# A hybrid decoder layer on one core: norm and rotation of a projection put between the next projection's products, and half of the first expert query put behind the first head's keys

## The chip, the core and the metric

The kernel runs on one core of a Trainium2 chip, as one launch. The metric is the device time of that launch in microseconds (us), taken as the median of several runs. The core has five engines with a queue of instructions each, which they work off in order: PE (TensorE, matmuls), DVE (VectorE), ACT (ScalarE), POOL (GpSimd) and SP (SyncE, which here only issues transfers). Transfers between the memory of the chip (HBM) and the core run on 16 DMA engines, whoever issued them. An instruction waits for others through semaphores.

## The reference

256 positions of width 1024 go through one layer. In short:

```python
h = rms_norm(x, attn_norm)
mq, mk, mv, dq, dk, dv = split(h @ w_in)               # six projections of 512 columns each
mq, mk, dq, dk = apply_rope(rms_norm(.., gain), cos, sin)   # per head of 64
a = moba_attention(mq, mk, mv)                          # 8 heads x 64, causal within 256
b = diff_attention(dq, dk, dv, lam)                     # 4 heads, (softmax1 - lam softmax2) V
x = x + concat(norm(a), norm(b)) @ w_out
# PEER: for each token 8 heads x 16 experts of 16384
q   = (xn @ w_query).reshape(.., 8, 2, 128)             # xn = rms_norm(x, ffn_norm)
sc  = einsum(q, sub_keys);  top_s, top_i = top_k(sc, 16)
best = top_k(top_s[0][:, None] + top_s[1][None], 16)    # 16 experts per head
act = gelu(xn . expert_down[e]);  x = x + sum(softmax(best) * act * expert_up[e])
```

## The kernel before

The 256 tokens are two blocks of 128, A and B. A token's place in its block is its partition. For block A everything up to the expert lists is computed first. Then the experts of A are fetched and added, one *slot* after another, and the attention of block B is computed in between, so that B's lists are there when A's experts are through. There are 256 slots, 128 for each block: a slot takes the same list position for all 128 tokens.

**A slot.** `issue()` puts an indirect transfer (a *gather*, line 605) on POOL's queue: it fetches for each token one row of 2048 floats, the down and the up vector of an expert, into a buffer `uv`, one MB in all. `dot()` (line 615) multiplies the down half with the token on DVE and sums it. `weigh()` (lines 621, 622, 627) makes gelu, gate and a diagonal matrix `dg` of the result on ACT. `add()` (line 639) multiplies `dg` with the up half on PE, into `acc`. In every fourth slot of block A the addition is on DVE instead (line 637). After that the buffer is free and `issue()` puts the next gather into it. So the number of buffers limits how many gathers are under way: four at first (`RING0`), five more (`gat1`) once the projections of block B are done and their memory is free, six more (`gat2`) once the attention of B is done. I count the gathers from 0.

**Lists.** `query()` (line 478) makes the queries of two heads (four products of 128 columns, 16 instructions each); `keys()` (line 489) multiplies one head's query with the keys; `route1()` and `route2()` search the 16 experts of a head on DVE (lines 511 to 576), and `ready` says how many gathers the lists allow. `choose(A, 0, 0, 1)` makes the first head's list, with which the first 16 gathers can start; `choose(A, 0, 1, 1)` makes the second head's.

**Block B in between.** A projection is `proj()` (line 185), eight products on PE into one bank `psB`, and `evac()`: ACT copies and squares the result (lines 196, 198), DVE sums the squares (201) and makes the inverse root in eleven small instructions (`rsqrt`, lines 124 to 134), POOL and DVE multiply with the rotation tables (215 on POOL, 217 on DVE), POOL adds the two (220) and DVE scales (222). The last three together with the root I call the *norm and rotation* of a projection. `turn()` (line 229) transposes the result on PE. The projections are numbered 5, 4 (values), 2, 3 (a key and a query), 0, 1 (the other query and key). Weights come in four tiles of 512 KB per projection through a ring of eight tiles (`WRING`), issued on SP by `fetch`.

**What sets the order.** Up to `manual_schedule()` a scheduler orders the instructions on each engine. From there on they stand as the program writes them: the main loop takes a slot, then so many steps of the generator `behind()` as `STEPS` says (four at first), and a step is what a generator does up to its next `yield`. `behind()` mixes the second head's list with `front()`, which holds projections 3, 0 and 1 of block B and then its attention.

## Time and profile before

| what | us |
|---|---|
| median of 3 runs (851.11 to 854.19) | 852.66 |
| the profiled execution | 848.25 |
| its span, first to last instruction | 846.5 |

PE is busy for 80% of the span, DVE for 63%, POOL for 48% and ACT for 35%. The profile page has a line that gives the mean busy share of the DMA engines in 40 slices of the span: it is 9 tenths or more in most of them, with a dip in the fourth and fifth slice (about 63 to 106 us) and another in the eighth and ninth (about 148 to 190 us). A row of a timeline gives the start, the duration, the engine, the source line, the operation with what it writes and reads, and in brackets how long its engine had been idle and what ended that.

### The profile page before, as it was taken

The numbers are of one execution on the slowest core, as the hardware profiler recorded it, in microseconds if no ns is written. First come the engines' busy times: TensorE is split into PE (matmuls) and PEld (weight loads), VectorE is DVE, ScalarE is ACT, GpSimd is POOL, SyncE is SP. The second block draws the span as 40 slices with busy tenths as digits, with TensorE's granted clock in tenths as the row PEclk, the third lists the DMA queues.
The fourth block names the chain that finished last, engine by engine and source line by source line (L and its number), as shares of the span: only waits on it lengthen the run. The fifth ranks groups of instructions, "written<-read, shape, count | busy, mean of one in ns | idle before, by whom it ended". The sixth has DMA issues, their size and how long they took to land.

```text
span 846.5 us, 8001 instructions
## 1 busy us (share of the span) xinstructions
PE 679.3 (80%) x2028; PEld 323.8 (38%) x2028; DVE 535.0 (63%) x1417; ACT 299.9 (35%) x907; POOL 410.4 (48%) x438
## 2 busy tenths in 40 slices
PE   6999987776988958986668767699787877878776
PEld 2454633253654723543425333244222222222222
DVE  4754566757878798676596868774454544545444
ACT  1331232313645534233243333443333333333332
POOL 3310343465447537455538384755555555555530
PEclk9999998878897989998898999889999999999999
DMA  9992798669899999999999999999999999999993
GB/s 350 352 356 91 244 409 332 230 263 406 302 395 376 369 409 382 420 417 419 420 418 420 417 419 420 421 420 420 420 418 421 420 421 418 420 421 420 420 419 155
DMA packets 51534, 318.93 MB, mean 377 GB/s; under 512 B 6113, under 2 KB 6369, under 8 KB 18593
## 3 DMA queue, kind: packets, MB, share of 16 engines
q0 software_dynamic: 36944, 268.85, 78.0%
q1 hardware_dynamic: 14112, 48.93, 15.2%
q10 hardware_dynamic: 432, 0.66, 0.2%
q8 instruction: 16, 0.26, 0.1%
q14 instruction: 30, 0.24, 0.1%
HBM read 317.36 MB, written 1.05 MB: 376 GB/s over the span
## 4 chain that ended last, share of the span: by engine, by line
DMA 43%; PE 31%; DVE 16%; issue 4%; ACT 3%; POOL 2%; DVEq 0%; POOLq 0%; SPq 0%; ACTq 0%
DMA uv<-in_uv_dram,eid 41%; PE acc L639 10%; PE psB L185 7%; PE psA L478 5%; DVE uv L615 5%; PE psB L353 3%; PE psA L255 1%; DMA w<-in_win_dram 1%; DVE x L637 1%; PE psA L489 1%; DMA w<-in_wout_dram 1%; DVE topi L514 1%; POOL uv L605 1%; DVE topi L523 1%; DVE s L517 1%
## 5 line engine op out<-in xcount | busy, mean ns | idle before, releaser
L639 PE MATMUL acc<-uv,dg 128*128 128x512 f32 x896 | 455.3, 639 | 129.2 <-ACT dg L627 123.5
L605 POOL DMA_INDIRECT uv<-in_uv_dram,eid x256 | 316.7, 1237 | 312.4 <-DMA uv<-in_uv_dram,eid 141.6
L615 DVE SCALAR_TENSOR_TENSOR uv<-uv,xn 128x1024 f32<-128x1024 f32 x256 | 311.1, 1227 | 163.7 <-DMA uv<-in_uv_dram,eid 161.2
L639 PEld LDWEIGHTS acc<-uv,dg 128*128 128x128 f32 x896 | 163.8, 199 | 379.2 <-ACT dg L627 233.6
L621 ACT ACTIVATE hdot<-hdot 128x1 f32<-128x1 f32 x256 | 51.3, 200 | 322.9 <-DVE uv L615 321.8
L627 ACT ACTIVATE dg<-ident,hdot 128x128 f32<-128x128 f32 x224 | 89.9, 401 | 21.2 <-PE acc L639 14.4
L185 PE MATMUL psB<-w,xT 128*128 128x512 f32 x192 | 89.8, 617 | 6.9 <-DMA w<-in_win_dram 6.9
L622 ACT ACTIVATE hdot<-hdot,gate 128x1 f32<-128x1 f32 x256 | 75.4, 294 | 8.3
L478 PEld LDWEIGHTS psA<-xgT,w 128*128 128x128 f32 x512 | 69.4, 207 | 21.3 <-issue 20.3
L478 PE MATMUL psA<-xgT,w 128*128 128x128 f32 x512 | 69.3, 289 | 0.0
L185 PEld LDWEIGHTS psB<-w,xT 128*128 128x128 f32 x192 | 37.2, 199 | 51.1 <-issue 49.1
L499 POOL TENSOR_TENSOR ci<-tf 128x4 f32<-128x4 f32 (+5 forms) x81 | 27.8, 375 | 55.6 <-DVE tf L527 55.5
L637 DVE SCALAR_TENSOR_TENSOR x<-uv,hdot,x 128x1024 f32<-128x1024 f32 x32 | 41.7, 1303 | 5.2 <-ACT hdot L622 5.2
L571 DVE TENSOR_REDUCE ef<-hit 128x16 f32<-128x320 f32 (+3 forms) x18 | 12.0, 670 | 37.5 <-POOL hit L557 37.5
L353 PE MATMUL psB<-w,mT 128*128 128x512 f32 x64 | 30.8, 610 | 2.7 <-DMA w<-in_wout_dram 2.7
L557 POOL TENSOR_TENSOR hit<-hit,ci 128x160 f32<-128x160 f32 (+1 forms) x32 | 27.0, 873 | 2.9 <-DVE hit L554 2.5
L215 POOL TENSOR_TENSOR qt<-pr,rS 128x128 f32<-128x128 f32 (+1 forms) x24 | 15.6, 675 | 24.1 <-ACT pr L196 24.0
L511 DVE MAX8 tops<-sc 128x8 f32<-128x128 f32 x32 | 7.2, 281 | 30.3 <-ACT sc L490 30.3
L615 DVE DVE_READ_ACCUMULATOR uv<-uv,xn 128x1 f32 x256 | 20.9, 82 | 0.0
L353 PEld LDWEIGHTS psB<-w,mT 128*128 128x128 f32 x64 | 12.0, 194 | 17.4 <-issue 13.2
L196 ACT ACTIVATE pr<-psB,r 128x512 f32<-128x512 f32 x8 | 5.5, 685 | 36.8 <-PE psB L185 31.2
L482 ACT COPY qs<-psA 128x512 f32<-128x512 f32 (+1 forms) x9 | 4.8, 536 | 36.6 <-PE psA L478 36.6
(126 smaller groups left out, 424.9 us busy)
## 6 DMA issues: line engine op xcount, KB each, us to landing
w<-in_win_dram SPq DMA_DIRECT2D x40, 512.0 KB, 7.3
w<-in_wq_dram SPq DMA_DIRECT2D x28, 512.0 KB, 11.8
w<-in_wout_dram SPq DMA_DIRECT2D x16, 512.0 KB, 11.3
uv<-in_uv_dram,eid POOLq DMA_INDIRECT x256
sk<-in_sk_dram SPq DMA_DIRECT2D x1, 1024.0 KB
out_dram<-x SPq DMA_DIRECT2D x4, 256.0 KB
xT<-in_xT_dram SPq DMA_DIRECT2D x2, 256.0 KB
x<-in_x_dram ACTq DMA_DIRECT2D x1, 512.0 KB
```

The costliest lines, as they stand in the source:

```text
L185: PE.matmul(p, lhsT=xT[tt][:, k], rhs=W[ci, tt][k // 2][:, k % 2], start=(k == 0), stop=(k == KC - 1))
L353: PE.matmul(wops[tt, n], lhsT=mixT[tt, MOBA if k < 4 else DIFF][:, k % 4], rhs=W["o", n, tt][k // 2][:, k % 2], start=(k == 0), stop=(k == ...
L478: PE.matmul(p[:, c], lhsT=w[k // 2][:, k % 2, c * P:(c + 1) * P], rhs=xgT[tt][:, k], start=(k == 0), stop=(k == KC - 1))
L499: eng.tensor_tensor(d, src[:, :, 1, b0:b0 + nb], src[:, :, 0, a0:a0 + 1].to_broadcast([P, src.shape[1], nb]), op=OP.add)
L557: G.tensor_tensor(e[:, h], e[:, h], ci[:, h, None, :n].to_broadcast([P, 8, n]), op=OP.mult)
L605: G.indirect_dma_start(out=rows[n], out_offset=None, in_=uv_d, in_offset=bass.IndirectOffsetOnAxis(ap=eid[tt][:, k:k + 1], axis=0))
L615: V.scalar_tensor_tensor(uv[:, :D], uv[:, :D], 1.0, xn[n // NSEL], op0=OP.mult, op1=OP.mult, accum_out=h)
L621: S.activation(h, h, AF.Gelu)
L622: S.activation(h, h, AF.Copy, scale=gate[n // NSEL][:, col:col + 1])
L627: S.activation(dg, ident, AF.Copy, scale=h)
L637: V.scalar_tensor_tensor(x2[tt], uv[:, D:], dg, x2[tt], op0=OP.mult, op1=OP.add)
L639: PE.matmul(acc[tt][:, c], lhsT=dg, rhs=uv[:, D + c * 512:D + (c + 1) * 512], start=(k == 0), stop=(k == NSEL - 1))
```

## The change

Three things are written in another order; no arithmetic is added or removed.

1. The first `query` is run for two of its four products, then the first head's list is made, and then the other two products are computed. The weights of the next query are fetched behind that.
2. The weights of projections 3, 0 and 1 of block B are fetched by lines of their own, ahead of where `project` had fetched them.
3. In `front()`, the steps of projection 0's products alternate with the steps of `evac` of projection 3 (and its turns), and those of projection 1's products with `evac` of projection 0. Only `evac` of projection 1 stands alone behind its products.

```diff
     load_q(0, wqp)
-    run(query(A, 0, ((0, 2), (2, 4))))
+    q0 = query(A, 0, ((0, 2), (2, 4)))
+    for _ in range(4):
+        next(q0)
+    run(choose(A, 0, 0, 1))
+    run(q0)
     load_q(1, wqp)
-    run(choose(A, 0, 0, 1))
...
     def project(g):
-        if g < 4:
+        if g == 2:
             fetch((g, B), win_d[g], wts)
         else:
             W[g, B] = W[g, A]
         yield from proj(g, B)
         yield from evac(g, B)
-        if g in (3, 1):
-            turn(g - 1, B)
-            yield
-            turn(g, B)
-            yield
 
     run(project(5), project(4), project(2))
+    fetch((3, B), win_d[3], wts)
+    fetch((0, B), win_d[0], wts)
...
-        for g in (3, 0, 1):
-            yield from project(g)
+
+        def turned(g):
+            yield from evac(g, B)
+            if g == 3:
+                turn(2, B)
+                yield
+                turn(3, B)
+                yield
+
+        yield from proj(3, B)
+        fetch((1, B), win_d[1], wts)
+        for g in (0, 1):
+            p, e = proj(g, B), turned(3 if g == 0 else 0)
+            next(p)
+            yield
+            for _ in p:
+                yield
+                next(e, None)
+                yield
+            for _ in e:
+                yield
+        yield from evac(1, B)
+        turn(0, B)
+        yield
+        turn(1, B)
+        yield
```

On SP's queue all rows stand as before: the transfers of the weights keep their places in the built program, although the lines that fetch them have moved. What moves is on the other engines. In the rows, `x2` is a count, and the numbers behind names tell buffers apart.

PE, from the last products of projection 3 (`psB_922`) on, before the change; `psB_1040` is projection 0, the two rows L229 are the turns of projections 2 and 3, and each L639 row is the add of a gather, here gathers 2, 3, 4 and 6:

```order
L185 MATMUL psB_922<-w_918,xT1_104 128x512 x2
L185 MATMUL psB_922<-w_920,xT1_104 128x512 x2
L639 MATMUL acc_935<-uv_899,dg_949 128x512 x2
L639 MATMUL acc_935<-uv_901,dg_966 128x512 x2
L229 MATMUL psA_1008<-ident_117,qo_880 128x128 x4
L229 MATMUL psA_1015<-ident_117,qo_989 128x128 x4
L639 MATMUL acc_935<-uv_938,dg_1000 128x512 x2
L185 MATMUL psB_1040<-w_1032,xT1_104 128x512 x2
L185 MATMUL psB_1040<-w_1034,xT1_104 128x512 x2
L185 MATMUL psB_1040<-w_1036,xT1_104 128x512 x2
L639 MATMUL acc_935<-uv_970,dg_1065 128x512 x2
```

The same place after the change, where projection 3 is `psB_930` and projection 0 is `psB_972`:

```order
L185 MATMUL psB_930<-w_893,xT1_104 128x512 x2
L185 MATMUL psB_972<-w_895,xT1_104 128x512
L639 MATMUL acc_943<-uv_915,dg_957 128x512 x2
L185 MATMUL psB_972<-w_895,xT1_104 128x512
L185 MATMUL psB_972<-w_897,xT1_104 128x512
L639 MATMUL acc_943<-uv_917,dg_980 128x512 x2
L185 MATMUL psB_972<-w_897,xT1_104 128x512
L639 MATMUL acc_943<-uv_946,dg_998 128x512 x2
L185 MATMUL psB_972<-w_899,xT1_104 128x512 x2
L185 MATMUL psB_972<-w_901,xT1_104 128x512
L229 MATMUL psA_1068<-ident_117,qo_880 128x128 x4
L639 MATMUL acc_943<-uv_984,dg_1060 128x512 x2
```

Seven of projection 0's eight products now stand ahead of the turns, and the add of gather 4 (`uv_946`) stands ahead of both turns.

DVE, around the norm of projection 0 (it begins with L201), before the change; `uv_1030` is gather 8, and the dot of gather 9 (`uv_1068`) follows eleven rows of the root, two of L217 and the three small rows L545, L547 and L549 further down:

```order
L538 MAX best_1098<-cs_1047 128x8
L540 MAX_INDEX pos_1099<-best_1098,cs_1047 128x8
L542 MATCH_REPLACE s3_1100<-best_1098,cs_1047 128x50
L615 SCALAR_TENSOR_TENSOR uv_1030,hdot_1104<-uv_1030,xn0_653 128x1024
L201 TENSOR_REDUCE ssq_1114<-sq_1096 128x8
L124 TENSOR_SCALAR rs_v_1117<-ssq_1114 128x8
```

The same place after the change; the dot of gather 9 reads `uv_1063`:

```order
L538 MAX best_1104<-cs_1042 128x8
L540 MAX_INDEX pos_1105<-best_1104,cs_1042 128x8
L542 MATCH_REPLACE s3_1106<-best_1104,cs_1042 128x50
L615 SCALAR_TENSOR_TENSOR uv_1030,hdot_1110<-uv_1030,xn0_653 128x1024
L545 MAX best_1104<-s3_1106 128x8
L547 MAX_INDEX pos_1105<-best_1104,s3_1106 128x8
L549 CAST posf_1128<-pos_1105 128x16
L615 SCALAR_TENSOR_TENSOR uv_1063,hdot_1130<-uv_1063,xn0_653 128x1024
L201 TENSOR_REDUCE ssq_1138<-sq_1123 128x8
```

The dot of gather 9 and the three small rows of the second list have moved ahead of the norm of projection 0.

POOL, from the gathers into the first freed buffers on, before the change (L605 are gathers 4 to 8):

```order
L605 DMA uv_938<-in_uv_dram,eid0_672 128x2048
L605 DMA uv_952<-in_uv_dram,eid0_672 128x2048
L605 DMA uv_970<-in_uv_dram,eid0_672 128x2048
L215 TENSOR_TENSOR qt_990<-pr_956,rS1_817 128x8x32 x2
L605 DMA uv_1004<-in_uv_dram,eid0_672 128x2048
L220 TENSOR_TENSOR qo_989<-qo_989,qt_990 128x512
L605 DMA uv_1030<-in_uv_dram,eid0_672 128x2048
```

The same place after the change:

```order
L605 DMA uv_946<-in_uv_dram,eid0_672 128x2048
L605 DMA uv_960<-in_uv_dram,eid0_672 128x2048
L605 DMA uv_984<-in_uv_dram,eid0_672 128x2048
L605 DMA uv_1002<-in_uv_dram,eid0_672 128x2048
L605 DMA uv_1030<-in_uv_dram,eid0_672 128x2048
L215 TENSOR_TENSOR qt_1034<-pr_987,rS1_817 128x8x32 x2
```

Gathers 7 and 8 now stand ahead of the rotation of projection 3; the sum of that rotation (L220) stands further down, behind the twelve small rows of the second list and behind gather 9. Up to the first gather into the five new buffers, POOL issues 17 gathers before the change and 18 after it.

## Rows read from the trace of the kernel before

**Rows 1.** The page: span; DMA queues with packets, MB and share of 16 engines' span.

```profile
span 846.5 us, 8001 instructions
...
q0 software_dynamic: 36944, 268.85, 78.0%
q1 hardware_dynamic: 14112, 48.93, 15.2%
```

**Rows 2.** Busy time by stretch: length, engines (instructions), then PE clock, DMA share, GB/s.

```profile
102.00:138.00 36.00, 27.09 (x65) 11.96 (x64) 23.52 (x71) 11.20 (x28) 15.72 (x15) 0.91 1.00 401
138.00:180.00 42.00, 30.09 (x69) 13.27 (x69) 28.58 (x68) 12.18 (x31) 22.85 (x34) 0.87 0.60 205
...
204.00:232.00 28.00, 24.32 (x108) 15.64 (x107) 23.57 (x57) 15.67 (x41) 15.79 (x20) 0.83 0.88 330
...
300.00:818.00 518.00, 403.98 (x1046) 174.23 (x1045) 325.80 (x791) 186.72 (x598) 284.45 (x278) 0.95 1.01 417
```

**Rows 3.** Timeline: the first query, the first head's keys, and gather 0.

```profile
85.18 7.46 PE L478 MATMUL psA<-xgT,w 128*128 128x128 f32 x64
...
92.48 0.61 PE L489 MATMUL psA<-sk,qs 128*128 128x128 f32 x4
...
102.27 1.05 POOL L605 DMA_INDIRECT uv<-in_uv_dram,eid  x1 [1.68 <-DMA w<-in_win_dram]
```

**Rows 4.** Timeline: the copy of projection 2, and the add of gather 0.

```profile
110.36 0.69 ACT L196 ACTIVATE pr<-psB,r 128x512 f32<-128x512 f32 x1 [6.24 <-PE psB L185]
...
114.32 1.98 PE L639 MATMUL acc<-uv,dg 128*128 128x512 f32 x4 [1.03 <-ACT dg L627]
```

**Rows 5.** Timeline of POOL: issues of gathers 8, 9, 17 and 18.

```profile
137.34 0.96 POOL L605 DMA_INDIRECT uv<-in_uv_dram,eid  x1 [6.31 <-DVE x L637]
141.36 0.96 POOL L605 DMA_INDIRECT uv<-in_uv_dram,eid  x1 [0.16 <-issue]
...
178.69 1.95 POOL L605 DMA_INDIRECT uv<-in_uv_dram,eid  x1 [0.30 <-issue]
180.94 0.94 POOL L605 DMA_INDIRECT uv<-in_uv_dram,eid  x1 [0.30 <-issue]
```

**Rows 6.** Timeline of PE: turn 3, adds 4 and next, projection 0.

```profile
132.87 1.08 PE L229 MATMUL psA<-ident,qo 128*128 128x128 f32 x4 [5.20 <-DVE qo L222]
133.75 3.62 PE L639 MATMUL acc<-uv,dg 128*128 128x512 f32 x4
...
137.16 5.92 PE L185 MATMUL psB<-w,xT 128*128 128x512 f32 x12
```

**Rows 7.** Timeline of DVE: dots 3, 4, 8, 9, 12; sums (L201) of projections 0 and 1.

```profile
122.97 1.23 DVE L615 SCALAR_TENSOR_TENSOR uv<-uv,xn 128x1024 f32<-128x1024 f32 x1 [0.46 <-DMA uv<-in_uv_dram,eid]
...
129.93 2.18 DVE L615 SCALAR_TENSOR_TENSOR uv<-uv,xn 128x1024 f32<-128x1024 f32 x1
...
142.84 1.23 DVE L615 SCALAR_TENSOR_TENSOR uv<-uv,xn 128x1024 f32<-128x1024 f32 x1 [2.60 <-DMA uv<-in_uv_dram,eid]
...
147.91 0.69 DVE L201 TENSOR_REDUCE ssq<-sq 128x8 f32<-128x512 f32 x1 [3.84 <-ACT sq L198]
...
148.83 1.93 DVE L125 TENSOR_SCALAR rsq<-rs_v 128x8 int32<-128x8 int32 x1
...
154.82 1.21 DVE L615 SCALAR_TENSOR_TENSOR uv<-uv,xn 128x1024 f32<-128x1024 f32 x1
...
163.27 1.22 DVE L615 SCALAR_TENSOR_TENSOR uv<-uv,xn 128x1024 f32<-128x1024 f32 x1
...
168.99 0.69 DVE L201 TENSOR_REDUCE ssq<-sq 128x8 f32<-128x512 f32 x1 [4.50 <-ACT sq L198]
```

**Rows 8.** Timeline of POOL: sum of rotation 3, first part of rotation 0.

```profile
129.76 1.26 POOL L220 TENSOR_TENSOR qo<-qo,qt 128x512 f32<-128x512 f32 x1 [1.28 <-DVE qo L217]
...
149.46 1.69 POOL L215 TENSOR_TENSOR qt<-pr,rS 128x128 f32<-128x128 f32 x4
```

**Rows 9.** Timeline of SP: issues of weight tiles.

```profile
94.84 26.11 SPq L92 DMA_DIRECT2D w<-in_win_dram  x14
```

## The prediction

> **What bounds the kernel now.** I began with the page's DMA queues. The gathers take 78.0% of the span on 16 engines, and there are 256 of them: 0.780 x 846.5 / 256 = 2.58 us for one, 660 us for all. The other queue's 48.93 MB take 15.2%, 128.7 us, or 1.38 us for a tile of 512 KB [rows 1]. Together that is 93% of the span. Next I read the busy time by stretch. From 300 to 818 us the DMA engines are busy throughout (share 1.01) [rows 2]: there no engine's speed matters, the end comes when the transfers are through. So an edit is worth only the time that the DMA engines lie free before 300, and a lead won there stays until the end. The stretches show where free time is: none from 102 to 138 (share 1.00), 0.40 x 42 = 16.8 us from 138 to 180, and 0.12 x 28 = 3.4 us from 204 to 232 [rows 2].
>
> Then I asked the timeline why gathers fail to come between 138 and 180. Four buffers are there, so gather n+4 or so is issued only when an earlier one has had its dot on DVE and its add. The reader is to see that DVE and PE stand still with the dots behind them. DVE idles for 3.84 us ahead of the sum of projection 0's squares at 147.91, because the products of projection 0 have only just ended; the whole norm follows, and the dot of gather 9, issued at 141.36, comes at 154.82 only [rows 5, 7]. For projection 1 it is the same, with 4.50 us of idle time ahead of 168.99 [rows 7]. PE stands for 5.20 us in front of the turn at 132.87, with the add of gather 4 and all of projection 0 behind it (first product 137.16) [rows 6]. The stage ends when the five new buffers open: their first gather, number 17, is issued at 178.69, number 18 at 180.94 [rows 5].
>
> **The change, part by part.** I measure the lead at gather 18, at equal gather number, since from there the DMA engines are nearly full in both kernels.
>
> *First list.* Half the query, 7.46 / 2 = 3.7 us of PE work, no longer stands ahead of the keys at 92.48, one product (0.9 us, a pair of records at 1.98 / 4 each) does [rows 3, 4]; so gather 0 may come some 2.6 us earlier than 102.27. I count that as nothing. The DMA engines are full from 102 on, and the next buffer comes free with the add of gather 0 at 114.32, which waits for ACT; ACT was held by the copy of projection 2 at 110.36, behind the same PE work as before [rows 2, 4]. The cover is this ACT row; without it 2.6 us would be won at most.
>
> *The moved fetches.* Nothing: SP's rows keep their order, and each waits for the product that frees its tile.
>
> *Until the norm of projection 0 begins.* Gather 8 waited 6.31 us on POOL for the DVE addition of gather 5, until 137.34 [rows 5]; that addition stood behind the norm of projection 3. Now it waits for the add of gather 4, which stands ahead of the turns. Landings follow each other at some 3.7 us around gather 3 (dot at 122.97, waited for the transfer) [rows 7], so gather 4 lands at 124.5 to 126.7; dot 1.23, ACT about 0.9, add 1.98 [rows 4, 7] bring gather 8 out at 129 to 131. On DVE the norm of projection 3 follows dot 4 and takes until about 130; dots 5 and 6 and the addition of gather 5 come behind it, 1.2 to 1.3 us each with small rows between, so that gather 9 is issued at 135 to 136 against 141.36. From the end of an issue to the landing it is 142.84 - 138.30 = 4.5 us when the queue is short [rows 5, 7], so gather 9 is there at 141 or 142, and its dot comes straight behind dot 8 and three small rows, at about 143 to 144.5 instead of 154.82. The norm of projection 0 follows it without a wait for the squares (its products end at about 137): begin about 145.2 instead of 147.91, **-2.7 us** (bounds -4 and 0).
>
> *From that norm to the norm of projection 1.* Before: 168.99 - 147.91 = 21.1 us. Dot 9 (1.2) and the three small rows ahead of it (an estimate of 1.4, a fifth of the 6.9 us between 147.91 and 154.82, which hold the norm and them) are gone from this stretch: -2.6. The wait for squares: 4.50 becomes what ACT needs behind dot 12, 0.9 + 2 x 0.69 = 2.3 [rows 4, 7]: -2.2. New is a wait on DVE in L222, which needs POOL's sum L220; that now stands behind gather 14, which waits for an add. Issue 0.96 and L220 1.26 with the hand-overs make about 3 us [rows 5, 8]: +3.0. Sum **-1.8 us** (bounds -5 and +2).
>
> *From there to gather 18.* Before: 180.94 - 168.99 = 11.95. After: the norm, dots 13 and 14, L220 and L222, one DVE addition, and gathers 17 and 18, some 11 to 13: **-0.5 us** (bounds -1.5 and +1). One gather more is out by then, which is what the equal number counts.
>
> *Port lock.* The dot at 129.93 took 2.18 us and not 1.23 while POOL's L220 ran (129.76 to 131.02); the small L125 took 1.93 us, over POOL's L215 at 149.46 to 151.15 [rows 7, 8]. The change puts POOL's rotations among the dots of other gathers. The Trainium skill ("SBUF — State Buffer", section "SBUF: two separate sides") says that DVE operations with two SBUF inputs and GpSimd operations take a shared port pair by exclusive lock, the loser blocked for the whole instruction; the trace agrees, 2.18 against 1.23 us. By that rule alone every L215 and L220 could cost a dot its length, and the sum would be the rival "eaten up" below. I leave the lock as it was, since DVE now stands in L222 for part of L220; bound: three rotations of 1.9 + 1.26 us all blocked, less what before pays in the two rows above (1.0 + 1.8): +6.7 us.
>
> *Behind gather 18.* Queries, lists and attention follow in the same order, shifted. The 3.4 us from 204 to 232 may go or double.
>
> Sum: 0 + 0 - 2.7 - 1.8 - 0.5 = -5.0 us. On the profiled execution, 848.25, that gives 843.25; this execution lies 4.4 us under the median of the runs, so for the median I take 852.66 - 5.0 = **847.7 us**.
>
> **The rivals.**
>
> *Eaten up (no change).* L222 waits on DVE twice (3 us each), and port locks of up to 6.7 us take the place of the waits that go. For it: DVE is a queue in order, and only 13.4 of 42 us from 138 to 180 were idle there (42 - 28.58) [rows 2]. Against it: DVE loses waits of 3.84, 2.60 and 2.2 us outright [rows 7]. Time: 847.7 + 5 = 852.7, give or take 2. Chance 0.22.
>
> *More.* PE's clock. After PE's wait of 5.20 us the four records of an add take 3.62 us, against 1.98 at 114.32 [rows 4, 6]: that is 1.2 in place of 2.4 GHz, and the mean granted clock from 138 to 180 is 0.87 [rows 2]. If the products of projection 0, now spread over the waits, keep PE from falling, adds and turns are 1.7 us shorter each time, and two or three of these lie on the path; with the 3.4 us of 204 to 232 partly gone the lead is about 10: 842.5. The Trainium skill ("TensorE: Matmul & The Clock Gate", section "HAM oscillation") says that idle gaps between groups of products throttle the clock; the trace agrees, 3.62 us after a gap. Against it: PE still waits in front of the last turn and of adds 10 and 12. Chance 0.14.
>
> *Slower.* Weights come too late. Projection 0's first product moves from 137.16 to about 120.6 (add of gather 0 ends at 116.3, then ten records of 0.43 us), and the adds of gathers 2, 3 and 4 stand behind it on PE. SP issued W2's last two, then projections 3, 0 and 1, four tiles each, from 94.84 to 120.95 [rows 9]. Between gather 0's issue at 102.27 and dot 3 at 122.97 lie 20.7 us of full DMA; four gathers take 10.3, the rest is 10.4 / 1.38 = 7.5 tiles [rows 1, 3, 7]. Evenly spread, projection 0's tiles land at 116, 119, 121.5 and 124.5; they are needed at 120.6, 123.5, 128 and 130. So there are some 4 us to spare. If the gathers went first instead, the first of these tiles would land behind 122.97 and five tiles: at about 130, PE would stand 9 us, and gathers 6 to 8 with it: 847.7 + 9.4 = 857. It decides from a delay of 8 us on, where the lead of 5 is spent and 2.6 lost. Chance 0.10.
>
> **How the numbers follow.** The forecast has 0.54, with its own range of 845 to 850.5. 0.3%, 2.6 us, is about what a measurement can tell from no change. Faster is the forecast and "more", a little less than 0.68 for the forecast's edge: 0.67. Same is "eaten up": 0.22; slower 0.11. The range leaves out the far half of "more" and the slower case: 841.5 to 853.
>
> **What would show it.** Right: the sum of projection 0's squares (L201) with no idle time for ACT ahead of it, dot 9 ahead of it; gather 8 issued at about 130; gather 18 at about 176; the DMA share from 138 to 176 near 0.7. The first list: gather 0 near 99.7, but gather 4 still at about 116.5. Wrong: idle time of PE at 120 to 130 until a transfer of weights; DVE idle in front of L222 for more than 6 us in all; gather 18 early but the DMA engines free behind 200 for longer than 3.4 us, so that the lead is given back.

## The result: slower by half a per cent, and the profile after

The changed kernel takes 855.93 us (median of 10 runs, 852.97 to 857.54), the kernel before 852.93 (10 runs, 847.33 to 854.19). The ratio is 1.0052 with an interval of 1.0031 to 1.0073: slower, by some 4 us (the two medians differ by 3.0). The forecast was 847.7 us, and 853 was the top of its range. The profiled execution took 855.98 us.

The page after (span; DMA queues with packets, MB and share of 16 engines' span), against [rows 1]:

```profile
span 854.2 us, 7999 instructions
...
q0 software_dynamic: 36944, 268.85, 77.2%
q1 hardware_dynamic: 14112, 48.93, 15.1%
```

As many bytes are moved, and the span is 7.7 us longer, so the DMA engines lie free for longer. The stretches after, against [rows 2] (columns as there: the last three are PE's granted clock, the DMA share and GB/s):

```profile
102.00:138.00 36.00, 31.29 (x77) 13.35 (x75) 22.01 (x61) 10.28 (x27) 16.12 (x16) 1.00 1.02 415
138.00:180.00 42.00, 27.41 (x64) 12.43 (x64) 27.51 (x80) 13.29 (x34) 21.70 (x33) 0.83 0.67 240
...
204.00:232.00 28.00, 23.40 (x96) 14.70 (x95) 21.41 (x54) 15.82 (x42) 12.98 (x18) 0.82 0.87 327
232.00:300.00 68.00, 56.27 (x247) 34.95 (x247) 53.05 (x151) 32.67 (x89) 33.83 (x38) 0.85 0.88 343
300.00:818.00 518.00, 405.51 (x1067) 176.62 (x1066) 323.48 (x790) 188.19 (x601) 286.54 (x279) 0.95 1.01 417
```

The same stretch from 232 to 300 in the kernel before, which the prediction did not look at:

```profile
232.00:300.00 68.00, 60.35 (x277) 37.41 (x276) 54.32 (x157) 34.55 (x101) 38.41 (x40) 0.92 0.98 383
```

From 138 to 180 the change wins a little (share 0.67 for 0.60, 2.9 us of transfers). From 232 to 300 it loses 0.10 x 68 = 6.8 us, in a place that the change does not touch.

**A clock for the comparison.** The program up to the first query is the same in all kernels here, yet in 18 profiled executions the query starts between 85.18 and 89.15 us: 85.18 before, 86.73 after. So I count times from its start. Two numbers then tell nearly everything: when gather 18 is issued, and the free DMA time, each stretch times one minus its DMA share. The table sums the free time over windows of 15 to 42 us, good to about 0.5 us each. Each row is one execution, and executions of one kernel differ by several us (the one of `after_sooner1` took 851.47 us, the median there is 847.38). "95 to 260" leaves out 180 to 200, which has its own column.

| kernel | gather 18 | free, 0 to 95 | 95 to 260 | 180 to 200 | span less start | ratio to before |
|---|---|---|---|---|---|---|
| before | 95.8 | 22.8 | 3.2 | 1.4 | 761.3 | 1 |
| after | 94.3 | 20.8 | 6.7 | 6.6 | 767.5 | 1.0052 |

The free time grows by 6.7 us and the span by 6.2: the loss is free DMA time, and most of it lies between 180 and 200 us behind the query's start, 267 to 287 us of the execution.

**Where the early lead stays.** POOL after (start, duration, line, operation, idle time before and what ended it): gathers 8 and 9, sum L220 of projection 3, gather 14, the sum of projection 0, gathers 17 and 18, against [rows 5]:

```profile
132.16 1.99 POOL L605 DMA_INDIRECT uv<-in_uv_dram,eid  x1 [1.69 <-PE acc L639]
...
139.90 0.98 POOL L605 DMA_INDIRECT uv<-in_uv_dram,eid  x1
140.90 1.27 POOL L220 TENSOR_TENSOR qo<-qo,qt 128x512 f32<-128x512 f32 x1
...
160.10 0.97 POOL L605 DMA_INDIRECT uv<-in_uv_dram,eid  x1 [0.16 <-issue]
161.09 1.27 POOL L220 TENSOR_TENSOR qo<-qo,qt 128x512 f32<-128x512 f32 x1
...
179.04 1.70 POOL L605 DMA_INDIRECT uv<-in_uv_dram,eid  x1 [3.34 <-DVE x L637]
181.05 0.95 POOL L605 DMA_INDIRECT uv<-in_uv_dram,eid  x1 [0.30 <-issue]
```

DVE after, the sums of squares (L201) of projections 0 and 1 and the scalings (L222) of 3, 0 and 1, against [rows 7]:

```profile
142.21 0.69 DVE L222 TENSOR_TENSOR qo<-qo,rsq 128x512 f32<-128x512 f32 x1 [4.04 <-POOL qo L220]
...
148.65 0.69 DVE L201 TENSOR_REDUCE ssq<-sq 128x8 f32<-128x512 f32 x1 [0.40 <-ACT sq L198]
...
162.39 0.69 DVE L222 TENSOR_TENSOR qo<-qo,rsq 128x512 f32<-128x512 f32 x1 [3.99 <-POOL qo L220]
...
167.80 0.69 DVE L201 TENSOR_REDUCE ssq<-sq 128x8 f32<-128x512 f32 x1 [2.19 <-ACT sq L198]
...
175.73 0.69 DVE L222 TENSOR_TENSOR qo<-qo,rsq 128x512 f32<-128x512 f32 x1 [2.91 <-POOL qo L220]
```

The waits for squares are gone or halved (3.84 to 0.40, 4.50 to 2.19 us), as intended. In their place DVE stands 10.9 us in front of L222, because POOL's sum L220 comes late. For projection 3 POOL is busy until 140.88 with the sums of the second list and with gather 9. For projections 0 and 1 the rotation L215, which goes ahead of L220, stands behind a gather that waits for an add (POOL idle for 2.65 us until 156.51 and for 6.82 us until 170.72). All dots behind L222 wait too.

**Where the loss is.** The second attention's scores (L252) are computed on PE in two blocks of two halves. Before, PE, ACT and POOL there:

```profile
263.42 3.70 PE L639 MATMUL acc<-uv,dg 128*128 128x512 f32 x8
267.05 0.48 PE L252 MATMUL psA<-qk,qk 64*128 64x128 f32 x2
268.43 0.49 PE L252 MATMUL psA<-qk,qk 64*128 64x128 f32 x2 [0.32 <-ACT ex L266]
...
271.60 3.61 PE L639 MATMUL acc<-uv,dg 128*128 128x512 f32 x4 [0.94 <-ACT dg L627]
...
267.24 0.23 ACT L562 ACTIVATE gate<-gate 128x32 f32<-128x32 f32 x1 [4.11 <-DVE gate L561]
267.37 0.46 ACT L266 ACTIVATE ex<-psA,mx 128x256 f32<-128x256 f32 x1
...
278.09 1.52 POOL L605 DMA_INDIRECT uv<-in_uv_dram,eid  x1 [1.66 <-PE acc L639]
```

The same after, with ACT, DVE and POOL:

```profile
266.32 1.98 PE L639 MATMUL acc<-uv,dg 128*128 128x512 f32 x4
...
273.85 0.79 PE L252 MATMUL psA<-qk,qk 64*128 64x128 f32 x2 [4.55 <-ACT ex L266]
...
275.51 3.78 PE L639 MATMUL acc<-uv,dg 128*128 128x512 f32 x4
279.23 0.79 PE L252 MATMUL psA<-qk,qk 64*128 64x128 f32 x2
...
268.97 0.23 ACT L562 ACTIVATE gate<-gate 128x32 f32<-128x32 f32 x1 [5.95 <-DVE gate L561]
269.22 1.28 ACT L621 ACT_TABLE_LOAD   x1
...
271.48 1.28 ACT L266 ACT_TABLE_LOAD   x1
272.77 0.47 ACT L266 ACTIVATE ex<-psA,mx 128x256 f32<-128x256 f32 x1
...
281.00 0.69 DVE L260 TENSOR_REDUCE mx<-psA 128x2 f32<-128x512 f32 x1 [3.42 <-PE psA L255]
...
285.04 1.28 DVE L637 SCALAR_TENSOR_TENSOR x<-uv,hdot,x 128x1024 f32<-128x1024 f32 x1
...
286.34 0.94 POOL L605 DMA_INDIRECT uv<-in_uv_dram,eid  x1 [5.83 <-DVE x L637]
```

The reader is to see a chain through four queues. PE waits 4.55 us with the second block for buffers that ACT's exponentials (L266) free; these come at 272.77 for 267.37 before, 3.9 us later when both are counted from the query's start. The gate's exponential L562 ahead of them is not late (182.2 us behind the query's start for 182.1): a dot's weighing and two more table loads (269.22 and 271.48) now stand between the two. An add stands behind that half on PE (275.51), and the block's other half behind the add. DVE waits 3.42 us for that half (L260), and the DVE addition behind it holds gather 48, which is issued 8.25 us later than before (278.09), 6.7 us counted from the query's start. PE's add at 275.51 takes 3.78 us for four records, against 1.98 at 266.32. In the 20 us from 266.73 on the granted clock is 0.66:

```profile
266.73:286.73 20.00, 15.45 (x48) 8.71 (x47) 14.91 (x31) 13.69 (x34) 8.39 (x8) 0.66 0.67 244
```

Before, in the same 20 us behind the query:

```profile
265.18:285.18 20.00, 18.74 (x86) 11.49 (x85) 17.68 (x38) 12.50 (x37) 12.18 (x12) 0.91 0.93 343
```

Why the order differs there: `front()` has two steps more ahead of the five new buffers, and the opening falls one gather later. So every later step stands one dot later. But every fourth slot of block A adds on DVE and puts no add on PE (gathers 17, 21, 25, ...; line 623), and these slots did not move. In the rows of the built programs, with D for the scores of one head (two heads make a half) and A for an add on PE, the order is `DD A DD AA DDDD A` before and `DD A DD A DD A DD` after: the slot without an add no longer falls into a block of scores.

### The profile page after: what moved, and what is told of

It is laid out like the page before. It is cut to its first block, busy times and chain, and to the rows that moved or that the text cites. A ratio compares the mean times of both kernels' runs of the same rounds, so it can differ in the third digit from the quotient of the medians.

```text
span 854.2 us, 7999 instructions
## 1 busy us (share of the span) xinstructions
PE 683.5 (80%) x2028; PEld 325.6 (38%) x2028; DVE 530.5 (62%) x1417; ACT 302.8 (35%) x909; POOL 412.1 (48%) x438
## 4 chain that ended last, share of the span: by engine, by line
DMA 46%; PE 29%; DVE 9%; POOL 7%; issue 6%; ACT 2%; POOLq 0%; DVEq 0%; SPq 0%; ACTq 0%
DMA uv<-in_uv_dram,eid 45%; PE acc L639 8%; PE psB L185 8%; PE psA L478 5%; DVE uv L615 3%; PE psB L353 3%; POOL uv L605 2%; POOL ci L499 2%; PE psA L255 2%; POOL hit L557 1%; DMA w<-in_wout_dram 1%; POOL qt L215 1%; DVE x L637 1%; DMA w<-in_win_dram 1%; PE psA L489 1%
## 5 line engine op out<-in xcount | busy, mean ns | idle before, releaser
L639 PE MATMUL acc<-uv,dg 128*128 128x512 f32 x896 | 456.4, 640 | 120.7 <-ACT dg L627 118.1
L605 POOL DMA_INDIRECT uv<-in_uv_dram,eid x256 | 317.0, 1238 | 326.4 <-DMA uv<-in_uv_dram,eid 136.0
L639 PEld LDWEIGHTS acc<-uv,dg 128*128 128x128 f32 x896 | 163.8, 199 | 368.8 <-ACT dg L627 228.3
L627 ACT ACTIVATE dg<-ident,hdot 128x128 f32<-128x128 f32 x224 | 89.9, 401 | 21.7 <-PE acc L639 14.9
L478 PE MATMUL psA<-xgT,w 128*128 128x128 f32 x512 | 72.2, 296 | 4.7 <-DMA w<-in_wq_dram 4.7
L499 POOL TENSOR_TENSOR ci<-tf 128x4 f32<-128x4 f32 (+5 forms) x81 | 33.6, 445 | 53.1 <-DVE tf L527 53.0
L215 POOL TENSOR_TENSOR qt<-pr,rS 128x128 f32<-128x128 f32 (+1 forms) x24 | 15.3, 666 | 26.8 <-ACT pr L196 26.8
L557 POOL TENSOR_TENSOR hit<-hit,ci 128x160 f32<-128x160 f32 (+1 forms) x32 | 25.1, 817 | 0.5 <-DVE hit L554 0.4
L511 DVE MAX8 tops<-sc 128x8 f32<-128x128 f32 x32 | 7.2, 280 | 26.8 <-ACT sc L490 26.8
L353 PEld LDWEIGHTS psB<-w,mT 128*128 128x128 f32 x64 | 12.0, 194 | 18.2 <-issue 13.5
L255 PE MATMUL psA<-qk,qk 64*128 64x128 f32 x64 | 16.9, 355 | 0.0
```

Of the source, the lines that this page charges most:

```text
L255: PE.matmul(p[:, j, tt * P:], lhsT=qT[rows, hd // 2], rhs=qk[cq + 1, tt][rows, hd // 2], start=False, stop=True)
L353: PE.matmul(wops[tt, n], lhsT=mixT[tt, MOBA if k < 4 else DIFF][:, k % 4], rhs=W["o", n, tt][k // 2][:, k % 2], start=(k == 0), stop=(k == ...
L478: PE.matmul(p[:, c], lhsT=w[k // 2][:, k % 2, c * P:(c + 1) * P], rhs=xgT[tt][:, k], start=(k == 0), stop=(k == KC - 1))
L499: eng.tensor_tensor(d, src[:, :, 1, b0:b0 + nb], src[:, :, 0, a0:a0 + 1].to_broadcast([P, src.shape[1], nb]), op=OP.add)
L605: G.indirect_dma_start(out=rows[n], out_offset=None, in_=uv_d, in_offset=bass.IndirectOffsetOnAxis(ap=eid[tt][:, k:k + 1], axis=0))
L627: S.activation(dg, ident, AF.Copy, scale=h)
```

## The experiments

All ratios are to the kernel before, timed beside it on the same chip, with the 95% interval in brackets. Line numbers in edited kernels are some lines higher.

**Is it the place of the later steps?** One step taken sooner in the changed kernel puts all later steps back; one empty step in the kernel before puts them where the change has them. Only these lines differ:

```diff
         rate[0] = 1
+        owed[0] = 1
...
-        steps += STEPS[rate[0]]
+        steps += STEPS[rate[0]] + owed[0]
+        owed[0] = 0
```

```diff
         rate[0] = 1
+        for _ in range(1):
+            yield
```

> The changed kernel with one step of the background work more in the slot in which the five new buffers open; all steps behind it then fall between the same dots as in the kernel before. Theory A (the loss arises in the later steps: the exponential of the gate L562 and those of the second attention's scores L266 are parted by a dot, so ACT loads a table twice more and PE waits 4.55 us for L266): the idle DMA time at 270 to 290 us is gone, and the time is that of the kernel before or a little under, 850 to 854 us. Theory B (the loss arises before 180 us: the second half of the first query delays weights, and DVE waits in L222 for POOL): the time stays at 855 to 857 us.

> The kernel before with one empty step of the background work behind the opening of the five new buffers; nothing else differs, and all later steps fall between the same dots as in the changed kernel. Theory A: L562 and L266 are parted as in the changed kernel, PE waits for L266, and the time is 3 to 8 us longer: 856 to 861 us. Theory B: an empty step costs nothing, 852 to 854 us.

Measured: 847.38 us, 0.997 (0.9949 to 0.999), and 859.12 us, 1.0102 (1.0058 to 1.0147). Theory A holds both ways as to the place of the later steps; the cause that it names, the parted exponentials and their table loads, is taken up further down. A single empty step, with no work in it, makes the kernel before 1% slower, and with the steps put back the same change is faster by 0.3%. Free time from 180 to 200: 1.8 and 4.2 us. So in `before_later1` only 2.8 of the 12.1 us by which the free time grows lie in the second attention's scores; the rest is spread over the other stretches. The first came out below the expected 850: the kernel before ran at 850.1 in that comparison.

**The two parts of the change.** `between` and `between_sooner1` undo the halved query and keep the interleaving; `first_list` does the opposite:

```diff
-    q0 = query(A, 0, ((0, 2), (2, 4)))
-    for _ in range(4):
-        next(q0)
-    run(choose(A, 0, 0, 1))
-    run(q0)
+    run(query(A, 0, ((0, 2), (2, 4))))
     load_q(1, wqp)
+    run(choose(A, 0, 0, 1))
```

> The changed kernel with the first query done whole ahead of the first head's keys, as before; the products of projections 0 and 1 stay between the norms of the projections ahead of them. Theory A: the later steps fall as in the changed kernel, so 855 to 857 us, the order of the first query counting for nothing. Theory B, where the halved query is to blame: 852 to 854 us, and the DMA share from 92 to 102 us is back at about 0.95; where the waits in L222 are to blame: 855 to 857 us.

> The kernel before with the first query halved around the first head's keys and nothing else. Theory A: gather 0 comes about 1 to 2.6 us earlier and gather 4 where it was (116 to 118 us), later steps as before: 852 to 854 us, no change. Theory B, where the halved query is to blame: the DMA share from 92 to 102 us falls to about 0.67 and 2 to 3 us are lost for good: 855 to 856 us.

> The interleaved products alone (first query whole, ahead of the first head's keys) with the later steps falling as in the kernel before. If the interleaving is worth what the first traces give at gather 18, counted from the start of the first query (94.6 against 95.8 us): about 1 us less than the kernel before, 848 to 850 us. If it is worth the forecast 5 us: 844 to 846 us. If the waits in L222 eat it up wholly: 850 to 852 us.

Measured: `between` 855.24, 1.0064 (1.0036 to 1.0091); `first_list` 847.51, 0.997 (0.9952 to 0.9988); `between_sooner1` 848.27, 0.9947 (0.9919 to 0.9974). The interleaving brings the misplaced steps with it. The halved query alone wins 0.3%, where both theories of that run gave it nothing or a loss. The interleaving, with the steps put back, wins 0.5%: gather 18 comes 1.4 us earlier, and the free time to 260 falls by 2.5 us (24.9 for 27.4). Both together (`after_sooner1`) win no more than either: 0.3%.

**The waits in L222.** POOL's rotation needs no root, so it can go ahead of it; then L220 stands a slot ahead of L222 (for projections 3, 0 and 1 of block B):

```diff
-        V.tensor_reduce(ss, sq, axis=AX.X, op=OP.add)
-        yield
-        rsqrt(rs, ss, 8, HD)
-        yield
...
         rotate()
+        V.tensor_reduce(ss, sq, axis=AX.X, op=OP.add)
         yield
         G.tensor_tensor(o, o, t, op=OP.add)
         yield
+        rsqrt(rs, ss, 8, HD)
+        yield
+        yield
         V.tensor_tensor(o, o, bc(rs, HD), op=OP.mult)
```

`rot_early` does it in `after_sooner1`, `rot_between` in `between_sooner1`, `rot_alone` in the kernel before, `first_rot` in `first_list`.

> The changed kernel with the later steps falling as in the kernel before (one step sooner), and with POOL's rotation L215 and sum L220 of projections 3, 0 and 1 ahead of the norm's reciprocal root, so that L222 no longer stands right behind them. If the waits in L222 (4.04, 3.99 and 2.91 us in the changed kernel) eat up the lead of the interleaving: these waits fall under 1 us each, gather 18 comes 3 to 5 us earlier, 842 to 845 us. If the stage is held by the adds and the landings anyway: 846 to 848 us, as without this edit.

> The interleaved products alone (first query whole), later steps as before, with POOL's rotation L215 and sum L220 ahead of the reciprocal root, so that L222 does not wait. If the interleaving is worth what the forecast gave it once these waits are gone: gather 18 comes 4 to 5 us earlier, counted from the start of the first query (91 to 92 us against 95.76), ratio 0.991 to 0.994. If its worth is what it showed with the waits: 94 to 94.5 us at gather 18, ratio 0.995 to 0.997.

> The kernel before with POOL's rotation L215 and sum L220 ahead of the reciprocal root in projections 3, 0 and 1, nothing else. DVE waits in L222 only once there, 1.15 us. If the rotation's place matters only where the interleaving makes L222 wait: gather 18 0 to 1.2 us earlier, ratio 0.998 to 1.001. If the earlier rotation is good by itself: 2 us or more, ratio under 0.998.

> The kernel before with the first query halved and POOL's rotation ahead of the reciprocal root, without the interleaved products. If the interleaving has a worth of its own beside these two (free DMA time of 10.9 us between gather 8 and gather 18's places with all three, 13.4 with the rotation alone): ratio 0.995 to 0.997, 1 to 3 us above the kernel with all three (0.9931). If it has none: 0.993, the same.

Measured: `rot_early` 846.43, 0.9931 (0.9905 to 0.9956), the fastest kernel here; `rot_between` 846.85, 0.994 (0.9914 to 0.9965); `rot_alone` 849.85, 0.9981 (0.9954 to 1.0008); `first_rot` 849.82, 0.9983 (0.9957 to 1.0008). In `rot_early` the three scalings have no idle time ahead of them:

```profile
138.02 0.68 DVE L234 TENSOR_TENSOR qo<-qo,rsq 128x512 f32<-128x512 f32 x1
...
159.25 0.69 DVE L234 TENSOR_TENSOR qo<-qo,rsq 128x512 f32<-128x512 f32 x1
171.10 0.69 DVE L234 TENSOR_TENSOR qo<-qo,rsq 128x512 f32<-128x512 f32 x1
```

and gather 18 comes 5.3 us earlier than before. Its time is a little above the expected 842 to 845 (the profiled execution took 842.62). But the rotation alone moves gather 18 by 4.2 us, more than expected, although in the kernel before DVE waited in L222 only once, 1.15 us. POOL shows another gain there: in the kernel before, its sum for projection 1 waited for DVE's half of the rotation (L217, first row), and in `rot_alone` the same sum does not (L228, second row):

```profile
174.70 2.11 POOL L220 TENSOR_TENSOR qo<-qo,qt 128x512 f32<-128x512 f32 x1 [2.46 <-DVE qo L217]
...
172.10 1.28 POOL L228 TENSOR_TENSOR qo<-qo,qt 128x512 f32<-128x512 f32 x1
```

The ratio of `rot_alone` does not differ from 1 for sure. `first_rot` came out above both values that were expected of it. With the rotation moved, the interleaving makes 0.9983 into 0.9931 and 0.9981 into 0.994, about 4 us, in separate comparisons. At gather 18 it is then worth 2.8 us with the whole query (91.5 to 88.7) and loses 1.5 us with the halved one (89.0 to 90.5).

| kernel | gather 18 | free, 0 to 95 | 95 to 260 | 180 to 200 | span less start | ratio to before |
|---|---|---|---|---|---|---|
| after_sooner1 | 93.9 | 21.8 | 4.8 | 1.8 | 762.8 | 0.997 |
| before_later1 | 96.4 | 23.6 | 11.7 | 4.2 | 774.3 | 1.0102 |
| between | 94.6 | 20.7 | 7.7 | 5.0 | 767.0 | 1.0064 |
| first_list | 93.3 | 21.0 | 2.2 | 1.4 | 759.6 | 0.997 |
| between_sooner1 | 94.4 | 20.7 | 2.8 | 1.4 | 758.4 | 0.9947 |
| rot_early | 90.5 | 17.2 | 3.1 | 1.4 | 755.0 | 0.9931 |
| rot_between | 88.7 | 16.3 | 7.8 | 0.4 | 756.6 | 0.994 |
| rot_alone | 91.5 | 19.3 | 8.2 | 3.2 | 763.7 | 0.9981 |
| first_rot | 89.0 | 18.2 | 5.5 | 1.8 | 758.0 | 0.9983 |
| joined | 94.2 | 21.4 | 6.4 | 3.6 | 763.6 | 1.0013 |
| after_later2 | 94.4 | 21.1 | 9.0 | 5.2 | 771.9 | 1.0059 |
| before_behind | 94.1 | 21.8 | 5.5 | 3.4 | 766.0 | 1.0047 |
| rot_behind | 89.8 | 18.2 | 7.5 | 0.6 | 760.0 | 0.9953 |
| after_add2 | 94.3 | 21.0 | 3.2 | 2.8 | 759.7 | 0.9975 |
| before_add2 | 95.7 | 22.6 | 3.4 | 1.0 | 761.3 | 0.9981 |
| before_add0 | 94.7 | 21.7 | 8.3 | 4.8 | 769.4 | 1.0086 |

**What in the place costs? First ACT.** In the changed kernel a dot's weighing stands between L562 and L266, with two more table loads. `joined` moves the gate's exponential behind the scores' ones; `after_later2` adds two empty steps, after which the two are neighbours again; `before_behind` and `rot_behind` swap the two without moving a step.

```diff
-        S.activation(g, g, AF.Exp)
+        if (tt, c4) != (A, 2):
+            S.activation(g, g, AF.Exp)
...
         yield from route1(tt, c4, h0, nh)
+        if (tt, c4) == (A, 2):
+            g = rs1[tt, c4, h0][1]
+            S.activation(g, g, AF.Exp)
         yield
```

```diff
+            while defer:
+                g = defer.pop()
+                S.activation(g, g, AF.Exp)
```

(the second stands in `scores`, right behind L266; `route1` puts this one gate into `defer`).

> The changed kernel with the exponential of the third query's gate (L562) one route step later, so that on ACT it stands behind the four exponentials of the second attention's scores (L266) with no table load between them; all else falls as in the changed kernel. Theory T (the two table loads between L562 and L266, 2 x 1.28 us, and what they hold up are the price): most of the loss is gone, 848 to 851 us. Theory O (the price is that the exponentials stand behind a dot's weighing and PE's next scores and adds behind them, whatever the tables): 853 to 856 us, and PE still waits over 3 us for L266 near 270 us.

> The changed kernel with two empty steps behind the opening of the five new buffers: all later steps come later still, but L562 and L266 fall between the same two dots again, as in the kernel before. Theory T and theory O (where the steps fall to the dots is what counts, not how late they are): 847 to 851 us, PE's wait for L266 under 1 us. Theory L (each step later costs time): 857 us or more.

> The kernel before with one instruction moved: on ACT the exponential of the third query's gate (L562) stands directly behind the four exponentials of the second attention's scores (L266) and not ahead of them. Theory W (what counts is that L266, which frees the buffers of PE's next scores, stands in ACT's queue behind L562, which waits for DVE): in the kernel before L562 waited 4.11 us, until 267.24, so L266 comes 1 to 2.5 us earlier and 1 to 2.5 us are won: 0.998 of the kernel before, about 850 to 852 us. Theory T (only the table loads between L562 and L266 count, and in the kernel before there are none): no change, 0.999 to 1.001.

> The changed kernel with later steps as before and POOL's rotation ahead of the reciprocal root (ratio 0.9931 to the kernel before), and L562 directly behind L266 too. Theory W: 1 to 2.5 us less, a ratio of about 0.991. Theory T: unchanged, about 0.993.

Measured: `joined` 853.57, 1.0013 (0.9991 to 1.0036); `after_later2` 856.70, 1.0059 (1.0029 to 1.009); `before_behind` 854.75, 1.0047 (1.0024 to 1.007); `rot_behind` 847.13, 0.9953 (0.9927 to 0.9979). Theories T and O fall with `after_later2`, for which both expected 847 to 851: L562 and L266 are neighbours there, and nothing comes back (an add stands on PE in every gap of the scores there too). The time is near the 857 of theory L; `after_add2` and `before_add0` below, which move no step, speak against that one. `joined` lies between theories T and O: PE no longer waits for L266, some 3 us of the 5 come back between 180 and 200, and the ratio is 1.0013 for 1.0052. That speaks for what stands between the two exponentials as a part of the price. But the same swap in the kernel before wins 3.4 us from gather 44 to 48 and loses more around it, 0.5% in all: theory W was right on the spot and wrong on the sum. In `rot_behind` it was wrong as well (0.9953 for the expected 0.991).

**Then PE.** `after_add2` moves the slots that add on DVE one later, as the steps have moved; `before_add2` does it in the kernel before; `before_add0` moves them one earlier there. No step moves and no instruction is added:

```diff
+    def on_dve(n):
+        return n < NSEL and n % DVE_ADD == (1 if n < 17 else 2)
...
-        if n < NSEL and n % DVE_ADD == 1:
+        if on_dve(n):
```

(`before_add0`: `1 if n < 14 else 0`).

> The changed kernel with the slots that add on DVE moved on by one from gather 17 on (gathers 18, 22, 26, ... in place of 17, 21, 25, ...), as the later steps have moved on by one; no step is moved. In the kernel before, the two halves of each attention's scores on PE fell into a slot whose add is on DVE, so no add on PE stood between them; in the changed kernel an add does. Theory M (this is the price: PE's queue stands in front of a half of the scores that waits for the exponentials L266, with adds behind it): 847 to 850 us, a ratio of 0.995 to 0.999, as with the later steps put back. Theory T (the two table loads between L562 and L266, which stay as in the changed kernel): 855 to 857 us, 1.004 to 1.007. Theory L (each later step comes a dot later): the same, 1.004 to 1.007.

> The kernel before with the slots that add on DVE moved on by one from gather 17 on; no step is moved. Now an add on PE stands between the halves of the scores, while L562 and L266 stay next to each other. Theory M: slower by what one empty step cost or a little less, a ratio of 1.004 to 1.010. Theories T and L: no change, 0.998 to 1.002.

> The kernel before with the slots that add on DVE one earlier from gather 14 on (gathers 16, 20, 24, ... in place of 17, 21, 25, ...); no step is moved. This gives the order of the changed kernel on PE, an add between any two parts of the second attention's scores, which moving them one later did not give. Theory M (the place of the steps to the slots that add on DVE): slower, a ratio of 1.004 to 1.010, with 5 us or more of free DMA time between 180 and 200 us behind the first query's start, against 1.4 in the kernel before. Theories T and L: no change, 0.998 to 1.002.

Measured: `after_add2` 847.59, 0.9975 (0.9951 to 0.9998); `before_add2` 848.96, 0.9981 (0.9959 to 1.0003); `before_add0` 858.98, 1.0086 (1.0055 to 1.0118). The middle one is a miss of theory M as I had put it: moved one later, the slot without an add falls into the first block of scores (`DDDD AA DD A DD`), and that costs nothing either, although an add now stands between the halves of the second block; PE waits 1.25 us for L266 there. Moved one earlier it falls into neither block, which is the changed kernel's order on PE, and the loss is there, with no step moved (4.8 us free from 180 to 200, where theory M had 5 or more). PE and ACT in `before_add0`:

```profile
274.24 0.79 PE L252 MATMUL psA<-qk,qk 64*128 64x128 f32 x2 [3.62 <-ACT ex L266]
...
275.91 3.73 PE L642 MATMUL acc<-uv,dg 128*128 128x512 f32 x4
...
273.05 0.23 ACT L562 ACTIVATE gate<-gate 128x32 f32<-128x32 f32 x1 [7.35 <-DVE gate L561]
```

PE waits for L266 as in the changed kernel, but L266 is late in another way: directly behind L562, which itself waits 7.35 us for DVE, where the first block's scores come later and an addition (269.92) now stands ahead of L561. And 3.4 of the 8.0 us by which the free time grows lie between 180 and 200. So what the runs show is that the place of the steps to the slots that add on DVE costs the time; they do not single out PE, ACT or DVE as the queue on which it is lost.

## Why the prediction was wrong

**The frame held.** The DMA engines are full from 300 us on in both kernels, and what is lost or won before stays to the end: over the 18 kernels of the tables the span less the start is 734 us plus the free time, within 3 us.

**The step that failed is "behind gather 18".** I took it that queries, lists and attention follow in the same order, shifted, and gave this a term of zero. They were shifted by one dot against a pattern of four that stayed, the slots that add on DVE. That costs about 1% by itself (1.0102 in `before_later1`, 1.0086 in `before_add0`), and without it the change gives 0.997 (`after_sooner1`, `after_add2`), some 2.5 us of the 5.0 that were forecast. The rows of the built program that the forecast had at hand show the shift. I read them only up to gather 18. The sign I had named, a lead given back behind 200 us, is what came, but not in the 3.4 us from 204 to 232: it came from 267 to 287. So the DMA engines were not nearly full in both kernels behind gather 18, as I had put it: from 232 to 300 their share was 0.98 before and 0.88 after.

**First list, worth 0: mis-sized.** It is worth 0.3%, about 2.5 us (`first_list`). Gather 0 comes 2.7 us earlier, and gather 4 at 31.40 us behind the query's start in both kernels, as I said: the cover, ACT's copy, is there. But it covers one gather. Gathers 1 to 3 land earlier as well, and gather 5 is issued at 33.8 for 36.8.

**The moved fetches, nothing: right.** PE waited for weights of the next projections 0.36 and 0.84 us, at 114.34 and 121.27. The rival "slower" needed 8.

**Until the norm of projection 0, -2.7: mis-sized.** L201 came at 148.65, and with the later start of the query taken off that is -0.8. Gather 8 was on time (132.16 less 1.55 is 130.6), gather 9 was not (139.90 less 1.55 is 138.4, not 135 to 136). I had not put in the scaling of projection 3, whose L220 stands behind gather 9 and POOL's list sums: 4.04 us.

**From that norm to the next, -1.8: right**, 21.1 to 19.15 us. Here I had counted the wait in L222 with 3.0; it was 3.99.

**From there to gather 18, -0.5: wrong sign**, 11.95 to 13.25 us, with the third L222 wait of 2.91. Together -1.4 instead of -5.0. The waits in L222 came to 10.9 us, where I had set 6 as the mark, so "eaten up" was the true rival for the stage, as far as these waits go. That they alone ate a lead of 5 us is not shown: in `rot_early`, without them, gather 18 comes 5.3 us earlier, but 4.2 of that come with `rot_alone` too, which has no interleaving. Nor would the forecast's size have held with another order of the rotation: the interleaving then moves gather 18 by 2.8 us (`rot_between`) or not forward at all (`rot_early` against `first_rot`).

**Open.** Why the swap of L562 and L266 helps after the change and hurts before it is not settled, nor why the halved query adds nothing to the interleaving (0.997 with it, 0.9947 without), nor to the earlier rotation (0.9983 for 0.9981). I can name what varies (PE's clock, POOL's sums, below), not what decides it. One rival stands untested: the profiled execution of `before_behind` has the slow sums described below and 2.6 us of free time behind them, so its loss may come from there and not from the swap.

## What to carry to other kernels

A hand-written schedule that interleaves two step sequences has a phase. Before costing a change of a few steps, compare the built order of every later stage and not only of the stage that is edited, above all against anything periodic; an empty step is the cheapest test. And where a wait is taken from one queue, look for what a neighbouring queue now holds in front of the same instruction: here the squares became free, and the sum on POOL behind gathers took their place, until the rotation, which needs no root, was moved ahead.

## What the hardware showed that I had not expected

**PE's clock prolongs a wait.** After its 4.55 us of idle time PE ran at the lower of its two levels, 1.2 GHz: the add behind took 3.78 us, against 1.98 ahead of the wait, and the granted clock over that stretch (third number from the end) is 0.50:

```profile
273.80:279.20 5.40, 5.35 (x9) 2.28 (x9) 2.76 (x7) 4.27 (x13) 1.85 (x2) 0.50 0.51 159
```

The kernel before has one such add as well (3.61 us at 271.60), but over the 20 us its granted clock is 0.91 and not 0.66. The Trainium skill ("PSUM — Partial Sum Buffer", section "Engine vs sequencer instructions") says that matmuls start and complete in program order; the trace agrees, since the add at 275.51 came only behind the half of the scores that waited.

**POOL's small sums can double.** The 12 sums of a list's indices (L511 and L513 there, L499 and L501 in the kernel before) took 7.3 us in `rot_alone`:

```profile
319.28 1.81 POOL L511 TENSOR_TENSOR ci<-tf 128x16 f32<-128x16 f32 x4
321.05 0.19 POOL L513 TENSOR_TENSOR ci<-tf 128x8 f32<-128x8 f32 x1
321.21 2.84 POOL L511 TENSOR_TENSOR ci<-tf 128x16 f32<-128x16 f32 x5
324.01 2.50 POOL L513 TENSOR_TENSOR ci<-tf 128x6 f32<-128x6 f32 x2
```

and 3.6 us in the kernel before, for the same list:

```profile
319.30 1.15 POOL L499 TENSOR_TENSOR ci<-tf 128x16 f32<-128x16 f32 x4
320.41 0.20 POOL L501 TENSOR_TENSOR ci<-tf 128x8 f32<-128x8 f32 x1
320.57 1.83 POOL L499 TENSOR_TENSOR ci<-tf 128x16 f32<-128x16 f32 x5
322.35 0.37 POOL L501 TENSOR_TENSOR ci<-tf 128x6 f32<-128x6 f32 x2
```

The gather behind them came 3.6 us later, counted from the query's start, and DVE then waited 5.56 us for POOL's L569; in that execution 3.2 us of DMA time were free between 240 and 260 us behind the query, where the kernel before has none. DVE's dots over the slow sums kept their 1.21 to 1.28 us. The Trainium skill ("SBUF — State Buffer", section "Who interferes with whom") says that the issue order decides which of DVE and GpSimd blocks where both want the port pair that they share, and that the one blocks fully. The trace agrees as far as POOL is the one that pays here; that the pair is what it waits for is not shown.

It is no oddity of `rot_alone`. From the start of the first to the end of the last, the sums of this list take 7.2 us in eight of the 18 profiled executions (`after_sooner1`, `before_later1`, `after_later2`, `before_behind`, `before_add0`, `rot_alone`, `rot_between`, `rot_behind`) and 3.2 to 4.9 us in the ten others. The eight have 2.6 to 4.6 us of free DMA time between 227 and 260 us behind the query, the ten 1.0 at most. So a part of the column "95 to 260" comes with these sums. Whether an edit brings them on, whether one kernel has both kinds of execution, and whether that is why some executions of one kernel differ by 3 us and more, no trace here shows.
